# Padding the sample's narrow matmuls and transposes to the full 128 x 128 array in a two-layer attention encoder

## The chip, the core and the metric

One core of one Trainium2 chip runs the whole program in one launch. The metric is device time in microseconds (us). The kernel before takes 1110.06 us, the median of 3 runs (1109.81 to 1110.37).

## What is computed

320 tokens of width 2048 go through two layers: 256 tokens of a prompt and 64 tokens of a sample, whose 128 earlier tokens lie in caches. Cut to what matters:

```python
# layer 0, 16 heads: latent attention, block-causal mask
s = (q . k) * 192**-0.5                  # 128 plain + 64 rotary dimensions
o = softmax(mask(s)) @ v
# layer 1, 16 heads: stick-breaking attention, strictly causal
z = (q . k) * 128**-0.5
log_fail = where(causal, log_sigmoid(-z), 0)
later = cumsum_from_the_right(log_fail) - log_fail
a = where(causal, exp(log_sigmoid(z) + later), 0)
o = a @ v
# both layers
x = x + (o * silu(gate)) @ w_o
```

A sample token attends to 128 past keys and to the 64 own keys of the sample. Those 64 rows and columns are what the change is about. The outputs are the normalised tokens and the new cache entries of both layers.

## The kernel before, in words

Activations are kept transposed, features on the 128 partitions and the 320 tokens along the free axis. Every weight tile is loaded by DMA, split by ScalarE (the high half, L72) and VectorE (the low half, L73), and used in three products in the type float32r: high x high, high x low, low x high (L84, L85, L87; L124 to L126 and L456 to L462 in layer 0). A matmul in plain float32 (own sample keys, own sample values, the last rows of the prompt) is issued as two instructions; the trace therefore counts 32 where there are 16 heads. A transpose is one instruction on TensorE with an identity matrix.

The work of a head is cut into steps in a queue (`steps`); `tick()` takes up one step after each piece of a product, so that the softmax of one head goes on while TensorE works on the products of another. A scheduler in the framework sets the final order of each engine's instructions, close to the order of the program.

Layer 0, `mla_head` (L330), per head:
- `scores` (L335): the scores of the prompt into a PSUM tile `sc`, those of the sample (64 rows, L341) into a part of the PSUM tile `o`; then the softmax. The sample's probabilities lie in `pq`, 64 partitions x 192 keys.
- `transposes` (L371): three full transposes of `p` (L375), then two of `pq`: L376 has 64 rows and 128 columns, L377 64 rows and 64 columns. ScalarE copies the results into `pt` (L382, and L383 for the 64 x 64 corner).
- `values` (L386): three float32r products, then plain float32: L391 (prompt), L392 (sample x past) and L393 (sample x own, contraction over 64 rows).

The own values of the sample lie in `vv[0:TS, 2]`, filled by L468 for each pair of heads.

Layer 1, `sb_head` (L522), per head:
- `scores` (L526): three float32r products (L529), then plain float32: L530 (past keys), L531 (own keys, 64 columns of the array), L532. VectorE clears the 64 rows of the PSUM tile that L531 leaves out (L533); then the softplus chain of ScalarE and VectorE (L535 to L542).
- `sums` (L545): L548 and L551, then two full transposes of `vT` (L560) and one of its last 64 columns (L561); ScalarE copies the results into `vt` (L565, L566).
- `values` (L569): L573 in float32r, then plain float32 L574, L575 (past values) and L576 (own values). `vt` holds zeros in the 64 rows without a key, so L576 has 128 rows already.

```python
pe.transpose(tr[:, 384:448], pq[:, TS:192], ident_t[0:TS, 0:TS])
pe.matmul(o[:, TP:T], vv[0:TS, 2, vs], pt[0:TS, 192:256], start=False, stop=True)
pe.matmul(sc[0:TS, 448:512], kT[:, TP:T], q[:, TP:T], start=False, stop=False)
pe.transpose(tr[0:TS, 256:384], vT[:, TP:T], ident_t)
```

Of the kernel before, what the change touches and what calls it, by code (L numbers as in the profile page):

```python
# [10 lines left out]
F32 = mybir.dt.float32  # L11
F32R = mybir.dt.float32r
AF = mybir.ActivationFunctionType
ALU = mybir.AluOpType
# [3 lines left out]
P = 128  # L18
TP, TS, PAST = 256, 64, 128
T = TP + TS  # L20
# [15 lines left out]
def stream_encoder(  # L36
# [21 lines left out]
    # Work that waits for other engines is cut into steps; one is taken up after each piece of a product.  # L58
# [45 lines left out]
    def gemms(srcs, xh, xl):  # L104
        """The products of a list of tiles, in order; the first three begin together with their first halves,
        so that the last columns of the input may come later."""
        outs = [bank() for _ in srcs[:3]]
        raws = [load(w) for w in srcs[:3]]
        for out, raw in zip(outs, raws):
            half(out, raw, 0, xh, xl)  # L110
        while steps:
            tick()
        for out, raw in zip(outs, raws):
            half(out, raw, 1, xh, xl)
            yield out
        for w in srcs[3:]:
            yield gemm(w, xh, xl)
# [34 lines left out]
    def sum_squares(pool, src, i, acc, name):  # L152
        """acc += src^2"""
        if i == 0:
            s.activation(acc, src, AF.Square)
            return
        sq = pool.tile([P, T], F32, name=name, bufs=2)
        s.activation(sq, src, AF.Square)
        v.tensor_tensor(out=acc, in0=acc, in1=sq, op=ALU.add)

    def inv_rms(pool, ps, n, name, keep=const):
        """1 / sqrt(ps / n + EPS) by the tables and one Newton step."""
        ms = pool.tile([P, T], F32, name="ms")
        r = keep.tile([P, T], F32, name=name)
        t = pool.tile([P, T], F32, name="mt")
        s.activation(t, ps, AF.Ln, bias=eps, scale=1.0 / n)
        s.activation(r, t, AF.Exp, scale=-0.5)
        v.tensor_scalar(ms, ps, 1.0 / n, EPS, op0=ALU.mult, op1=ALU.add)
        v.tensor_tensor(out=t, in0=r, in1=r, op=ALU.mult)
        v.scalar_tensor_tensor(out=t, in0=t, scalar=-0.5, in1=ms, op0=ALU.mult, op1=ALU.mult)  # L170
        v.scalar_tensor_tensor(out=r, in0=t, scalar=1.5, in1=r, op0=ALU.add, op1=ALU.mult)
        return r
# [22 lines left out]
    # ================= layer 0: latent attention =================  # L195
    xh = apool.tile([P, KT, T], F32R, name="ah")
    xl = apool.tile([P, KT, T], F32R, name="al")
    with ExitStack() as stack:
        mp = stack.enter_context(tc.tile_pool(name="mla", bufs=1, reuse_waits="tile"))
        with tc.tile_pool(name="mla_a", bufs=1, reuse_waits="tile") as pa:  # L200
            # The first three tiles go through the inner dimension in step with the arrival of x.
# [60 lines left out]
            # rotary keys: KA = [high; high], KB = [low; chunk mask], against QA = [high; low], QB = [high; chunk]  # L262
# [17 lines left out]
            # rotary key: 64 columns, so that [high | low] of a tile of weights fills the array  # L280
# [43 lines left out]
        # the sample's own latents as [high | low], whose products lie in the two halves of the rows  # L324
# [4 lines left out]

        def mla_head(h, qn, qh, ql, QA, QB, kn, kh, kl, vh, vl, vv, c0):  # L330
            """One head in three steps: scores and softmax, transposes, values."""
# [3 lines left out]
            def scores():  # L335
                sc = pss.tile([P, 512], F32, name="sc")
                o = pso.tile([P, 512], F32, name="o")
                for out, q0, q1, k0, k1 in (
                    (sc[:, 0:128], 0, P, 0, P),
                    (sc[:, 128:384], P, TP, 0, TP),  # L340
                    (o[0:TS, T:512], TP, T, TP, KV),  # L341
                ):
                    q, k = slice(q0, q1), slice(k0, k1)
                    if q0 == 0:
                        pe.matmul(out, qn[:, q], kn, start=True, stop=False)
                    else:
                        q_ = slice(q0 - P, q1 - P)
                        pe.matmul(out, qh[:, q_], kh[:, k], start=True, stop=False)
                        pe.matmul(out, qh[:, q_], kl[:, k], start=False, stop=False)
                        pe.matmul(out, ql[:, q_], kh[:, k], start=False, stop=False)  # L350
                    pe.matmul(out, QA[:, q], KA[:, k], start=False, stop=False)
                    pe.matmul(out, QB[R, q], KB[R, k], start=False, stop=True)
                nm = pb.tile([P, 4], F32, name="nm", bufs=2)
                sm = pb.tile([P, 4], F32, name="sm", bufs=2)
                p = pb.tile([P, 384], F32, name="p", bufs=2)
                pq = pb.tile([TS, 192], F32, name="pq", bufs=2)
                parts = (
                    (p[:, 0:128], sc[:, 0:128], P, 0),
                    (p[:, 128:384], sc[:, 128:384], P, 1),
                    (pq, o[0:TS, T:512], TS, 2),  # L360
                )
                for dst, src, n, i in parts:
                    v.tensor_reduce(out=nm[:n, i : i + 1], in_=src, axis=AX.X, op=ALU.max, negate=True)
                    s.activation(dst, src, AF.Exp, bias=nm[:n, i : i + 1], accum_out=sm[:n, i : i + 1])
                v.reciprocal(sm[:, 0:2], sm[:, 0:2])
                v.reciprocal(sm[:TS, 2:3], sm[:TS, 2:3])
                for dst, src, n, i in parts:
                    v.tensor_scalar(dst, dst, sm[:n, i : i + 1], None, op0=ALU.mult)
                at.update(o=o, p=p, pq=pq)

            def transposes():  # L371
                p, pq = at["p"], at["pq"]
                tr = pst.tile([P, 512], F32, name="tr")
                for j in range(3):
                    pe.transpose(tr[:, j * P : (j + 1) * P], p[:, j * P : (j + 1) * P], ident_t)  # L375
                pe.transpose(tr[:, 384:448], pq[:, TS:192], ident_t[0:TS, 0:TS])  # L376
                pe.transpose(tr[0:TS, 448:512], pq[:, 0:TS], ident_t[0:TS, 0:TS])  # L377
# [4 lines left out]
                s.copy(pt[:, 0:192], tr[:, 256:448])  # L382
                s.copy(pt[0:TS, 192:256], tr[0:TS, 448:512])  # L383
                at.update(ph=ph, pl=pl, pt=pt)

            def values():  # L386
# [4 lines left out]
                pe.matmul(o[:, P:TP], vv[:, 0, vs], pt[:, 0:128], start=False, stop=True)  # L391
                pe.matmul(o[:, TP:T], vv[:, 1, vs], pt[:, 128:192], start=True, stop=False)  # L392
                pe.matmul(o[:, TP:T], vv[0:TS, 2, vs], pt[0:TS, 192:256], start=False, stop=True)  # L393
# [6 lines left out]
        for pair in range(H // 2):  # L400
# [48 lines left out]
            vv = pb.tile([P, 3, 256], F32, name="vv", bufs=2)  # L449
# [32 lines left out]
    # ================= output projection, residual, input of layer 1 =================  # L482
# [15 lines left out]
    # ================= layer 1: stick-breaking attention =================  # L498
    # columns of a score tile: keys 0..127 x queries 0..255 | past x sample | keys 128..255 x queries 128..255 |
    # own x sample (in the first 64 rows; the others hold zeros, which are masked)  # L500
# [10 lines left out]
    kTs, vts = [], []  # L511
    for i in range(2):
        kT = sb.tile([P, T], F32, name=f"kT{i}")
        kTs.append(kT)
        vt = sb.tile([P, 2, P], F32, name=f"vt{i}")
        v.memset(vt[TS:P, 1, :], 0.0)
        vts.append(vt)
# [4 lines left out]
    def sb_head(h, q, qh, ql, kT, kh, kl, vT, g, vt, kp, vp):  # L522
        """One head in three steps: scores and their softplus, sums over later keys, values."""
        at = {}

        def scores():  # L526
# [4 lines left out]
            pe.matmul(sc[0:TS, 448:512], kT[:, TP:T], q[:, TP:T], start=False, stop=False)  # L531
            pe.matmul(sc[:, 320:448], kT[:, P:TP], q[:, P:TP], start=False, stop=True)  # L532
            v.memset(sc[TS:P, 448:512], 0.0)  # L533
# [11 lines left out]
        def sums():  # L545
# [13 lines left out]
            for j in range(2):  # L559
                pe.transpose(tr[:, j * P : (j + 1) * P], vT[:, j * P : (j + 1) * P], ident_t)  # L560
            pe.transpose(tr[0:TS, 256:384], vT[:, TP:T], ident_t)  # L561
# [3 lines left out]
            s.copy(vt[:, 0, :], tr[:, 128:256])  # L565
            s.copy(vt[0:TS, 1, :], tr[0:TS, 256:384])  # L566
            at.update(a=a, pairs=((vh, ah), (vh, al), (vl, ah)))

        def values():  # L569
            a = at["a"]  # L570
# [13 lines left out]
    for h in range(H):  # L584
# [15 lines left out]
        kT, vt = kTs[h % 2], vts[h % 2]  # L600
# [6 lines left out]
        vT = sb.tile([P, T], F32, name="vT", bufs=2)  # L607
        g = sb.tile([P, T], F32, name="g", bufs=2)
        f0, f1, f2 = sb_head(h, q, qh, ql, kT, kh, kl, vT, g, vt, kp[:, h % 4, :], vp[:, h % 4, :])
        steps.extend(([f0], [], [], [f1], [], [f2]))  # L610
        psv = gemm(wsb[4 * h + 2], xh, xl)
        v.tensor_tensor(out=vT, in0=psv, in1=r1, op=ALU.mult)
        nc.gpsimd.dma_start(ov[h], vT)
# [5 lines left out]
    # ================= output projection, residual, final norm =================  # L619
# [54 lines left out]
def _tiles(w):  # L674
    """[K, M] -> [M / 128, partition, K / 128 * 128]: a tile's weights in one run a partition."""
# [69 lines left out]
```

## Time and profile before

| what | value |
|---|---|
| median of 3 runs | 1110.06 us |
| span of the profiled execution, first to last instruction (its own time; no other is given for it) | 1108.3 us |
| TensorE matmul busy (PE) | 1087.4 us, 98% of the span |
| TensorE weight load busy (PEld) | 1072.9 us, 97% |
| VectorE busy (DVE) | 669.1 us, 60% |
| ScalarE busy (ACT) | 582.8 us, 53% |
| DMA queues, largest share of 16 engines | 39.5% |

Busy time of PE is a union of modelled durations: each matmul is shown for some 0.2 to 0.5 us, while the next one starts earlier. So a busy PE can still lose time, and what one matmul costs is read from the distance between the starts of two.

### The profile page before, as it was taken

What the parts mean: (1) busy time and instruction counts of PE and PEld (TensorE: products, weight loads), DVE (VectorE), ACT (ScalarE), POOL (GpSimd) and SP (SyncE); (2) the same over time, 40 slices, a digit from 0 to 9 for tenths busy, and PEclk for the clock granted to TensorE, in tenths of its full rate; (3) what the DMA queues carried; (4) which work ended last, traced back from release to release, by engine and by line L of the source; (5) the groups of instructions that cost most, each with busy time, mean ns of one, the idle gap of its engine ahead of it and who ended that gap; (6) DMA issues with size and microseconds to landing.
All of it is one profiled execution on the core that took longest, in us unless ns stands there. A gap on an engine that the chain in (4) does not pass through costs nothing.

```text
span 1108.3 us, 18683 instructions
## 1 busy us (share of the span) xinstructions
PE 1087.4 (98%) x7484; PEld 1072.9 (97%) x7484; DVE 669.1 (60%) x1355; ACT 582.8 (53%) x1260; POOL 18.8 (2%) x38
## 2 busy tenths in 40 slices
PE   7999999999999999999999999999999999999994
PEld 7999999999999999999999999999999999999994
DVE  7776556786877655555555555555555555555444
ACT  7755555665656544444555545545554545555441
POOL 0000000000000000000000000000000000000000
PEclk9999999999999999999999999999999999999997
DMA  8545443321312554444344443444343434434422
GB/s 304 169 161 185 153 152 100 111 96 58 115 58 77 197 198 169 169 149 156 125 159 151 159 152 138 162 142 154 131 164 127 164 131 160 134 145 153 152 77 95
DMA packets 30552, 159.41 MB, mean 144 GB/s; under 512 B 4264, under 2 KB 8304, under 8 KB 13952
## 3 DMA queue, kind: packets, MB, share of 16 engines
q1 hardware_dynamic: 26912, 151.01, 39.5%
q0 software_dynamic: 1712, 5.98, 1.5%
q10 hardware_dynamic: 1840, 1.22, 0.4%
q8 instruction: 58, 0.95, 0.3%
q14 instruction: 30, 0.25, 0.1%
HBM read 149.59 MB, written 8.60 MB: 143 GB/s over the span
## 4 chain that ended last, share of the span: by engine, by line
PE 97%; DMA 1%; DVE 1%; ACT 0%; issue 0%; DVEq 0%; SPq 0%; ACTq 0%
PE g L84 25%; PE g L87 25%; PE g L85 25%; PE g L124 3%; PE g L126 2%; PE g L125 2%; PE g L460 1%; PE g L461 1%; PE g L462 1%; PE sc L548 1%; PE sc L532 1%; DMA xt<-xT 1%; DVE x L640 1%; PE o L393 1%; PE o L573 1%; PE sc L529 1%
## 5 line engine op out<-in xcount | busy, mean ns | idle before, releaser
L72 ACT CAST whi<-raw 128x512 fp32r<-128x512 f32 (+1 forms) x539 | 309.4, 616 | 319.8 <-PE g L85 243.1
L73 DVE TENSOR_TENSOR wlo<-raw,whi 128x512 fp32r<-128x512 f32 (+1 forms) x539 | 353.3, 682 | 130.0 <-ACT whi L72 118.3
L84 PE MATMUL g<-x2h,whi 128*128 128x320 f32 x1024 | 305.9, 313 | 0.0
L85 PE MATMUL g<-x2l,whi 128*128 128x320 f32 x1024 | 302.1, 309 | 0.0
L84 PE MATMUL g<-ah,whi 128*128 128x320 f32 x848 | 250.9, 310 | 0.0
L85 PE MATMUL g<-al,whi 128*128 128x320 f32 x848 | 250.6, 309 | 0.0
L85 PEld LDWEIGHTS g<-x2l,whi 128*128 128x128 f32 x1024 | 192.4, 188 | 0.0
L84 PEld LDWEIGHTS g<-x2h,whi 128*128 128x128 f32 x1024 | 192.4, 188 | 0.0
L87 PE MATMUL g<-x2h,wlo 128*128 128x320 f32 x1024 | 171.0, 309 | 0.0
L85 PEld LDWEIGHTS g<-al,whi 128*128 128x128 f32 x848 | 159.2, 188 | 0.1
L84 PEld LDWEIGHTS g<-ah,whi 128*128 128x128 f32 x848 | 159.1, 188 | 0.2
L87 PEld LDWEIGHTS g<-x2h,wlo 128*128 128x128 f32 x1024 | 155.5, 188 | 0.0
L87 PE MATMUL g<-ah,wlo 128*128 128x320 f32 x848 | 141.6, 309 | 0.0
L87 PEld LDWEIGHTS g<-ah,wlo 128*128 128x128 f32 x848 | 128.7, 188 | 0.0
L627 DVE TENSOR_TENSOR x<-g,x 128x320 f32<-128x320 f32 x16 | 7.9, 492 | 37.5 <-PE g L87 37.5
L538 DVE SCALAR_TENSOR_TENSOR sp<-sc,sp 128x512 f32<-128x512 f32 x16 | 11.1, 691 | 31.9 <-ACT sp L537 31.9
L124 PE MATMUL g<-cq_h,whi 128*128 128x320 f32 x96 | 30.1, 314 | 0.0
L125 PE MATMUL g<-cq_l,whi 128*128 128x320 f32 x96 | 29.7, 309 | 0.0
L126 PE MATMUL g<-cq_h,wlo 128*128 128x320 f32 x96 | 29.7, 309 | 0.0
L149 ACT CAST ah<-og 128x320 fp32r<-128x320 f32 x32 | 14.7, 460 | 28.4 <-DVE og L395 17.6
L615 DVE TENSOR_TENSOR g<-g,r 128x320 f32<-128x320 f32 x16 | 7.9, 492 | 34.5 <-PE g L87 34.5
L460 PE MATMUL g<-whi,ckv_h 128*128 128x256 f32 x96 | 28.5, 297 | 0.0
(271 smaller groups left out, 1379.2 us busy)
## 6 DMA issues: line engine op xcount, KB each, us to landing
raw<-wsb SPq DMA_DIRECT2D x64, 1024.0 KB, 4.9
raw<-wo SPq DMA_DIRECT2D x32, 1024.0 KB, 4.9
raw<-win SPq DMA_DIRECT2D x21, 1024.0 KB, 5.0
raw<-wmla SPq DMA_DIRECT2D x12, 1024.0 KB, 4.9
xt<-xT SPq DMA_DIRECT2D x16, 160.0 KB, 2.7
ok<-kT POOLq DMA_DIRECT2D x16, 160.0 KB, 2.5
ov<-vT POOLq DMA_DIRECT2D x16, 160.0 KB, 2.1
raw<-win SPq DMA_DIRECT2D x3, 768.0 KB, 8.1
```

The costliest lines, as they stand in the source:

```text
L72: s.copy(hi[:, c], raw[:, c])
L73: v.tensor_tensor(out=lo[:, c], in0=raw[:, c], in1=f32(hi[:, c]), op=ALU.subtract)
L84: pe.matmul(out, hi[:, w], xh[:, k, :], start=k == 0, stop=False)
L85: pe.matmul(out, hi[:, w], xl[:, k, :], start=False, stop=False)
L87: pe.matmul(out, lo[:, i * P : (i + 1) * P], xh[:, k, :], start=False, stop=k == KT - 1)
L124: pe.matmul(out, hi[:, w], xh[:, k, :n], start=k == 0, stop=False)
L125: pe.matmul(out, hi[:, w], xl[:, k, :n], start=False, stop=False)
L126: pe.matmul(out, lo[:, w], xh[:, k, :n], start=False, stop=k == LT - 1)
L149: s.copy(hi, src)
L393: pe.matmul(o[:, TP:T], vv[0:TS, 2, vs], pt[0:TS, 192:256], start=False, stop=True)
L460: pe.matmul(out, ckv_h[:, k, ts], whi[:, w], start=k == 0, stop=False)
L538: v.scalar_tensor_tensor(out=sp, in0=sc, scalar=0.0, in1=sp, op0=ALU.max, op1=ALU.add)
```

## The change

- Layer 0: `pq` becomes two fixed tiles of 128 partitions whose lower 64 rows are set to zero once; the five transposes of a head all take 128 rows and 128 columns, in another order of columns, and overlap in the PSUM tile; one copy of 256 columns replaces the copies L382 and L383. `vv` becomes two fixed tiles whose lower 64 rows of the own values are set to zero once; L393 takes 128 rows.
- Layer 1: `kT` and `vT` become two fixed tiles each of 384 columns, the last 64 of them zero. L531 takes 128 columns of the array, L561 too. The clearing L533 goes. One copy of 256 columns replaces L565 and L566; `vt` becomes an ordinary tile with one buffer.
- The scores of the sample in layer 0 (L341, 64 columns of the array) and the products with 68 rows (L352) stay as they are.

```diff
+        pqs, vvs = [], []
+        for i in range(2):
+            pq = pb.tile([P, 192], F32, name=f"pq{i}")
+            v.memset(pq[TS:P, :], 0.0)
+            pqs.append(pq)
+            vv = pb.tile([P, 3, 256], F32, name=f"vv{i}")
+            v.memset(vv[TS:P, 2, :], 0.0)
+            vvs.append(vv)
...
-                for j in range(3):
-                    pe.transpose(tr[:, j * P : (j + 1) * P], p[:, j * P : (j + 1) * P], ident_t)
-                pe.transpose(tr[:, 384:448], pq[:, TS:192], ident_t[0:TS, 0:TS])
-                pe.transpose(tr[0:TS, 448:512], pq[:, 0:TS], ident_t[0:TS, 0:TS])
+                for c, src in ((0, p[:, 0:P]), (P, p[:, P:TP]), (TP, pq[:, 0:P]), (T, pq[:, TS:192]), (384, p[:, TP:384])):
+                    pe.transpose(tr[:, c : c + P], src, ident_t)
...
-                s.copy(pt[:, 0:192], tr[:, 256:448])
-                s.copy(pt[0:TS, 192:256], tr[0:TS, 448:512])
+                s.copy(pt, tr[:, 256:512])
...
-                pe.matmul(o[:, TP:T], vv[0:TS, 2, vs], pt[0:TS, 192:256], start=False, stop=True)
+                pe.matmul(o[:, TP:T], vv[:, 2, vs], pt[:, 0:64], start=False, stop=True)
...
-        kT = sb.tile([P, T], F32, name=f"kT{i}")
+        kT = sb.tile([P, 3 * P], F32, name=f"kT{i}")
+        v.memset(kT[:, T:], 0.0)
...
-            pe.matmul(sc[0:TS, 448:512], kT[:, TP:T], q[:, TP:T], start=False, stop=False)
+            pe.matmul(sc[:, 448:512], kT[:, TP:], q[:, TP:T], start=False, stop=False)
...
-            v.memset(sc[TS:P, 448:512], 0.0)
...
-            for j in range(2):
+            for j in range(3):
                 pe.transpose(tr[:, j * P : (j + 1) * P], vT[:, j * P : (j + 1) * P], ident_t)
-            pe.transpose(tr[0:TS, 256:384], vT[:, TP:T], ident_t)
...
-            s.copy(vt[:, 0, :], tr[:, 128:256])
-            s.copy(vt[0:TS, 1, :], tr[0:TS, 256:384])
+            vt = sb.tile([P, 2, P], F32, name="vt")
+            s.copy(vt.rearrange("p a c -> p (a c)"), tr[:, 128:384])
```

## Rows read from the trace of the kernel before

**Rows 1.** The page: span, TensorE, chain that ended last; then TensorE's longest wait.
```profile
span 1108.3 us, 18683 instructions
...
PE 1087.4 (98%) x7484; PEld 1072.9 (97%) x7484; DVE 669.1 (60%) x1355; ACT 582.8 (53%) x1260; POOL 18.8 (2%) x38
...
PE 97%; DMA 1%; DVE 1%; ACT 0%; issue 0%; DVEq 0%; SPq 0%; ACTq 0%
...
PE o L84 <- ACT whi L72: 6.1, 2, 5.8
```
**Rows 2.** Timeline of PE, layer 1 values of head 0 (start us, us, instruction).
```profile
515.19 0.39 PE L574 MATMUL o<-a,vt 128*128 128x128 f32 x2
...
515.58 0.39 PE L576 MATMUL o<-a,vt 128*128 128x64 f32 x2
...
516.01 0.30 PE L85 MATMUL g<-x2l,whi 128*128 128x320 f32 x1
```
**Rows 3.** Timeline of PE, layer 1 scores of head 0; then L531's durations, min/median/max.
```profile
495.39 0.33 PE L530 MATMUL sc<-q,kp 128*128 128x64 f32 x2
495.66 0.33 PE L531 MATMUL sc<-q,kT 128*64 128x64 f32 x2
495.91 0.49 PE L532 MATMUL sc<-q,kT 128*128 128x128 f32 x2
...
496.39 0.31 PE L85 MATMUL g<-x2l,whi 128*128 128x320 f32 x1
...
L531 PE MATMUL sc<-q,kT x32: 222/246/270, 495.7 to 966.5; 128*64 128x64 f32 x32
```
**Rows 4.** Timeline of PE, layer 0: last transpose and values of head 15.
```profile
374.12 0.22 PE L377 MATMUL tr<-ident_t,pq 64*64 64x64 f32 x1
...
376.48 0.38 PE L391 MATMUL o<-pt,vv 128*128 128x128 f32 x2
...
376.96 0.43 PE L393 MATMUL o<-pt,vv 64*128 64x64 f32 x2
...
377.57 0.31 PE L85 MATMUL g<-al,whi 128*128 128x320 f32 x1
```
**Rows 5.** Timeline of PE, layer 0 transposes of head 0.
```profile
210.09 0.49 PE L375 MATMUL tr<-ident_t,p 128*128 128x128 f32 x3
210.51 0.27 PE L376 MATMUL tr<-ident_t,pq 64*128 64x64 f32 x1
...
211.07 0.36 PE L125 MATMUL g<-ckv_l,whi 128*128 128x448 f32 x1
211.27 0.36 PE L126 MATMUL g<-ckv_h,wlo 128*128 128x448 f32 x1
```
**Rows 6.** Timeline of PE, layer 1 transposes of head 0.
```profile
507.46 0.38 PE L560 MATMUL tr<-ident_t,vT 128*128 128x128 f32 x2
507.68 0.27 PE L561 MATMUL tr<-ident_t,vT 128*64 128x128 f32 x1
...
507.94 0.30 PE L85 MATMUL g<-x2l,whi 128*128 128x320 f32 x1
```
**Rows 7.** Timeline of ACT and then of PE: layer 0 copies, layer 1 sums.
```profile
376.00 0.31 ACT L382 COPY pt<-tr 128x192 f32<-128x192 f32 x1
376.21 0.20 ACT L383 COPY pt<-tr 64x64 f32<-64x64 f32 x1
...
506.80 0.39 PE L548 MATMUL sc<-sph,triR 128*128 128x512 f32 x1
```
**Rows 8.** Timeline of DVE, layer 1 softplus of head 0.
```profile
496.61 0.11 DVE L533 MEMSET sc<- 64x64 f32 x1
...
501.05 0.68 DVE L150 TENSOR_TENSOR spl<-sp,sph 128x512 fp32r<-128x512 f32 x1
```
**Rows 9.** Timeline of PEld, weight loads of L531 and of L576, head 0.
```profile
495.65 0.19 PEld L531 LDWEIGHTS sc<-q,kT 128*64 128x64 f32 x2
...
515.52 0.30 PEld L576 LDWEIGHTS o<-a,vt 128*128 128x128 f32 x2
```

More of the change, by code (lines that the diff above doesn't have):

```diff
@@ L355, in scores @@
                 p = pb.tile([P, 384], F32, name="p", bufs=2)
-                pq = pb.tile([TS, 192], F32, name="pq", bufs=2)
+                pq = pqs[h % 2]
                 parts = (
@@ L359, in scores @@
                     (p[:, 128:384], sc[:, 128:384], P, 1),
-                    (pq, o[0:TS, T:512], TS, 2),
+                    (pq[0:TS, :], o[0:TS, T:512], TS, 2),
                 )
@@ L390, in values @@
                 pe.matmul(o[:, 0:TP], vl[:, vs], ph, start=False, stop=False)
-                pe.matmul(o[:, P:TP], vv[:, 0, vs], pt[:, 0:128], start=False, stop=True)
-                pe.matmul(o[:, TP:T], vv[:, 1, vs], pt[:, 128:192], start=True, stop=False)
-                pe.matmul(o[:, TP:T], vv[0:TS, 2, vs], pt[0:TS, 192:256], start=False, stop=True)
+                pe.matmul(o[:, P:TP], vv[:, 0, vs], pt[:, 128:256], start=False, stop=True)
+                pe.matmul(o[:, TP:T], vv[:, 1, vs], pt[:, 64:128], start=True, stop=False)
+                pe.matmul(o[:, TP:T], vv[:, 2, vs], pt[:, 0:64], start=False, stop=True)
                 og = pb.tile([P, T], F32, name="og")
@@ L448, in stream_encoder @@
             vl = pb.tile([P, 256], F32R, name="vl", bufs=2)
-            vv = pb.tile([P, 3, 256], F32, name="vv", bufs=2)
+            vv = vvs[pair % 2]
             for i, t0 in ((0, P), (None, 0), (2, None), (1, T)):
@@ L510, in stream_encoder, with sb_head @@
     s.activation(minusR, ones, AF.Copy, scale=-1.0)
-    kTs, vts = [], []
+    kTs, vTs = [], []
     for i in range(2):
-        kT = sb.tile([P, T], F32, name=f"kT{i}")
+        kT = sb.tile([P, 3 * P], F32, name=f"kT{i}")
+        v.memset(kT[:, T:], 0.0)
         kTs.append(kT)
-        vt = sb.tile([P, 2, P], F32, name=f"vt{i}")
-        v.memset(vt[TS:P, 1, :], 0.0)
-        vts.append(vt)
+        vT = sb.tile([P, 3 * P], F32, name=f"vT{i}")
+        v.memset(vT[:, T:], 0.0)
+        vTs.append(vT)
     oh = apool.tile([P, KT, T], F32R, name="ah")
     ol = apool.tile([P, KT, T], F32R, name="al")
-    def sb_head(h, q, qh, ql, kT, kh, kl, vT, g, vt, kp, vp):
+    def sb_head(h, q, qh, ql, kT, kh, kl, vT, g, kp, vp):
         at = {}
@@ L564, in sums @@
             plain_split(vh, vl, tr[:, 0:128])
-            s.copy(vt[:, 0, :], tr[:, 128:256])
-            s.copy(vt[0:TS, 1, :], tr[0:TS, 256:384])
-            at.update(a=a, pairs=((vh, ah), (vh, al), (vl, ah)))
+            vt = sb.tile([P, 2, P], F32, name="vt")
+            s.copy(vt.rearrange("p a c -> p (a c)"), tr[:, 128:384])
+            at.update(a=a, vt=vt, pairs=((vh, ah), (vh, al), (vl, ah)))
         def values():
-            a = at["a"]
+            a, vt = at["a"], at["vt"]
             o = pso.tile([P, 512], F32, name="o")
@@ L599, in stream_encoder @@
         plain_split(qh, ql, q[:, 0:TP])
-        kT, vt = kTs[h % 2], vts[h % 2]
+        kT, vT = kTs[h % 2], vTs[h % 2]
         psk = gemm(wsb[4 * h + 1], xh, xl)
@@ L606, in stream_encoder @@
         plain_split(kh, kl, kT[:, 0:P])
-        vT = sb.tile([P, T], F32, name="vT", bufs=2)
         g = sb.tile([P, T], F32, name="g", bufs=2)
-        f0, f1, f2 = sb_head(h, q, qh, ql, kT, kh, kl, vT, g, vt, kp[:, h % 4, :], vp[:, h % 4, :])
+        f0, f1, f2 = sb_head(h, q, qh, ql, kT, kh, kl, vT, g, kp[:, h % 4, :], vp[:, h % 4, :])
         steps.extend(([f0], [], [], [f1], [], [f2]))
         psv = gemm(wsb[4 * h + 2], xh, xl)
-        v.tensor_tensor(out=vT, in0=psv, in1=r1, op=ALU.mult)
-        nc.gpsimd.dma_start(ov[h], vT)
+        v.tensor_tensor(out=vT[:, 0:T], in0=psv, in1=r1, op=ALU.mult)
+        nc.gpsimd.dma_start(ov[h], vT[:, 0:T])
         psg = gemm(wsb[4 * h + 3], xh, xl)
```

## The prediction, written before the changed kernel was run

> **What bounds the kernel now.** I read the page first: the span is 1108.3 us, PE is busy for 98% of it, and the chain of work that ended last is PE for 97% [rows 1]. Then the waits of PE: the longest, 6.1 us, belongs to the first products (a weight half that is late at the start), and the heads have none [rows 1]. So TensorE sets the time, and a microsecond taken out of its stream of instructions comes off the end, as long as nobody makes it wait. Busy time can't show where that stream is thin, because the drawn matmuls overlap. So I read the timeline of PE around the instructions that the diff touches, and compare distances between starts.
>
> The measure is a block of the kernel before in which every matmul takes the whole array: the layer 1 values. From the first L574 to L85, the second matmul of the following product, it takes 516.01 - 515.19 = 0.82 us for six plain float32 instructions (two with 128 moving columns, four with 64) and one product matmul of 320 columns [rows 2].
>
> The layer 1 scores hold the same six shapes in another order, four with 64 moving columns and two with 128, and the same product behind, except that L531 loads only 64 columns of the array. From L530 to the second product matmul they take 496.39 - 495.39 = 1.00 us [rows 3]. The visible gap lies before L531 (0.27 us for two L530) and behind it. The 32 instructions of L531 have the same few durations from first to last [rows 3], so I take head 0 for all 16.
>
> The layer 0 values are again the same six shapes, but L393 takes 64 rows. From L391 to the second product matmul: 377.57 - 376.48 = 1.09 us [rows 4], which I take for all 16 heads too.
>
> The layer 0 transposes: from the first L375 to L125, the second matmul behind, 211.07 - 210.09 = 0.98 us; three transposes take 0.42 up to the start of L376, where the change of shape falls [rows 5].
>
> **The change part by part.**
>
> *Layer 1 scores.* After the change this is six full instructions and the product: 0.82 us by [rows 2] against 1.00, so 0.18 us a head, 16 x 0.18 = 2.9 us. L531's wider weights are inside the 0.82, since L576 loads 128 columns there.
>
> *Layer 0 values.* 1.09 - 0.82 = 0.27 us a head, 16 x 0.27 = 4.3 us. Most heads are followed by a product of 256 columns instead of 320, which shifts both sides alike.
>
> *Layer 0 transposes.* Full transposes come every 0.11 us: two L560 take 507.68 - 507.46 = 0.22 [rows 6]. Five take 0.55; the first product matmul behind them takes 0.20, as 211.27 - 211.07 shows for that shape [rows 5]. That is 0.75 against 0.98: 0.23 us a head, 3.7 us in all.
>
> *Layer 1 transposes.* L561 takes 64 columns before and 128 after. It follows L560 without a gap, and L85 comes 507.94 - 507.68 = 0.26 us later, one transpose of 0.11 and one product matmul of about 0.15 [rows 6]. Nothing is lost there now, so nothing is won: 0. The bound on the other side is a weight load twice as wide, 0.055 us by the difference in [rows 9], 0.9 us in all; the 0.11 us of the transpose in front of it covers that.
>
> At this place a rule can be weighed against a row. L561 shows no gap although its tile differs from its neighbours' [rows 6], while L376, L393 and L531 do. The Trainium skill, TensorEngine Tiling (Array Packing), Key Properties, says that changing the tiling mode drains the engine, and lists 128 x 64 as a mode of its own. By that, L561 would lose what the others lose, and padding it would win some 0.23 us a head more. The row says it does not; the sum goes by the row.
>
> *The sample's scores in layer 0* keep their 64 columns, so they neither cost nor win anything.
>
> *ScalarE.* L382 and L383 take 0.31 + 0.20 us [rows 7]; one copy of 256 columns lies between 0.31 and 0.51, and by columns near 0.37. L565 and L566 merge likewise. ScalarE is 53% busy and gets less to do: 0 for the path, apart from the last pair below. The single buffer of `vt` makes the copy of one head wait for L576 of the head before, which has run a whole head earlier: 0.
>
> *VectorE.* The 16 clearings L533 go, 0.11 us each [rows 8]. They stand ahead of the softplus chain, whose last result ends at 501.05 + 0.68 = 501.73 while L548, which reads it, starts at 506.80 [rows 7, 8]: over 5 us of cover, so their going gives 0. New are eight clearings at the start of the two layers, in place of two. At 0.11 to 0.3 us each (scaled from L533 by columns) they cost some 1.5 us of an engine that is idle 40% of the time: 0, at most that 1.5 if the low half of a weight queued behind them came late.
>
> *What is late next.* In the last pair of layer 0 the copies into `pt` end at 376.21 + 0.20 = 376.41 and L391 starts at 376.48 [rows 4, 7]: 0.07 us of margin. Between that head's transposes and its values lie the values of head 14, whose 0.27 us go. TensorE then comes too early and waits, in both heads of the pair. I put 0.2 us a head, 0.4 in all; the bounds are 0 (the merged copy is shorter) and 1.0. In the other pairs more products lie between the two steps.
>
> **Sum:** 2.9 + 4.3 + 3.7 - 0.4 = 10.5 us. The span goes from 1108.3 to 1097.8. The median of the runs is 1.8 us above the span, which I leave as it is: 1110.06 - 10.5 = **1099.6 us**, a gain of 0.9%.
>
> **The rivals.**
> 1. *Part of the gaps stays or comes back as waits.* Were the order of the last pair to shift so that PE waits out the whole chain from the last transpose, which starts at 374.12 [rows 4], to the end of the copies into `pt` at 376.41, 2.3 us, in both heads, 4.6 us would be lost instead of 0.4: 1103.8. For it: the margin of 0.07 us. Against: products stood between the steps before, and can again. 5%.
> 2. *More comes back.* If L561's narrow tile costs too and the 0.26 us hide it, 16 x 0.23 = 3.7 us more go: 1095.9. This is what the drain rule named above would give. Against: L561 starts 0.11 us after the transpose before it [rows 6]. 3%.
> 3. *The gaps do not hang on the shape.* They would then come from the change of type from float32r to float32 or from short matmuls, which stay, and the change does not do what it says: about 1110. Against: L574 to L576 have the same types and lengths, and no gap [rows 2]. 4%.
> 4. *Slower.* The gaps stay as in rival 3, and the wider weights show. Two loads of L531 take 0.19 us, two of 128 columns 0.30 [rows 9], so 0.11 more a head there, 0.055 for L377 and 0.055 for L561: 0.22 us a head, 3.5 us, 1113.6. It decides as soon as less than 0.22 us of gap goes per pair of heads (one of each layer), where the forecast has 0.68. The Trainium skill, TensorE: Matmul & The Clock Gate, LDWEIGHTS (loading the stationary operand), says that a load goes by its columns and not by its rows; the rows agree for columns. Against: in [rows 2] loads of 128 columns are in the 0.82 us already. 3%.
>
> **How the numbers follow.** The forecast has 85%, the rivals 15%. Starts are read to 0.01 us; over three blocks and 16 heads that is about half a microsecond. With the last pair's 0 to 1.0 us and 0.3 us between runs, the forecast's own range is 1098.4 to 1100.8. In the scores the two long instructions come last instead of first, which can hide one more load of 0.06 us a head, 1 us: down to 1097.4. Half of rival 1 takes the top to 1101.6. A measurement of this kernel tells 0.2%, 2.2 us, from no change. Forecast and rivals 1 and 2 are faster by more: 0.93. Rival 3 is the same: 0.04. Rival 4 is slower: 0.03.
>
> **What would show it.** Right: in the timeline of PE the layer 0 and layer 1 blocks each take 0.82 us up to the second product matmul, the five transposes start 0.11 us apart, the layer 1 transposes look as before, and PE waits only in the last pair of layer 0, for `pt` or `pl`. Wrong: L531 or L393 still start about 0.2 us after their neighbours; PE gets waits inside the heads; or the gaps are gone and the span has not shortened, which would mean that something beside TensorE paces the products.

## The result and the profile after

The changed kernel takes 1099.74 us (median; 1099.41 to 1099.97) where the kernel before takes 1110.21 (1109.81 to 1110.61) beside it: a ratio of 0.9905, 95% interval 0.9891 to 0.9919, so 10.5 us less. The forecast was 1099.6 us.

The page of the changed kernel, span and TensorE, then the chain that ended last, then TensorE's waits:

```profile
span 1097.6 us, 18604 instructions
...
PE 1076.9 (98%) x7484; PEld 1070.5 (98%) x7484; DVE 667.8 (61%) x1345; ACT 578.5 (53%) x1228; POOL 18.7 (2%) x38
...
PE 97%; DMA 1%; DVE 1%; ACT 0%; issue 0%; DVEq 0%; SPq 0%
...
PE o L84 <- ACT whi L72: 5.7, 1, 5.7
PE sc L630 <- ACT sq L640: 1.1, 1, 1.1
```

These answer to [rows 1]. TensorE executes as many matmuls as before, 7484, is as busy in share, and still bounds the kernel; its busy time went down by 10.5 us, as much as the runs did. Its count did not change, so the time came out of the distances between matmuls. Three starts split the span: the first product of layer 0's heads (L124), the first product of layer 1 (L84), and the sum of squares behind both layers (L624, in the changed kernel L630). Timeline of PE, before and then after:

```profile
183.93 0.31 PE L124 MATMUL g<-cq_h,whi 128*128 128x320 f32 x1
477.15 0.31 PE L84 MATMUL g<-x2h,whi 128*128 128x320 f32 x1
1093.94 0.81 PE L624 MATMUL sc<-sq,ones 128*128 128x320 f32 x2 [1.08 <-ACT sq L634]
```

```profile
183.44 0.31 PE L124 MATMUL g<-cq_h,whi 128*128 128x320 f32 x1
468.86 0.31 PE L84 MATMUL g<-x2h,whi 128*128 128x320 f32 x1
1082.94 0.81 PE L630 MATMUL sc<-sq,ones 128*128 128x320 f32 x2 [1.08 <-ACT sq L640]
```

Layer 0, from L124 to L84, went from 293.22 to 285.42 us, 7.8 less; layer 1, from L84 on, from 616.79 to 614.08, 2.7 less. Together that is the 10.5 us. The span fell by 10.8 us before rounding: another 0.5 us lie before L124, where the change touches nothing and where the profiles of this document differ by up to a microsecond (L124 starts between 183.28 and 184.25 us), and behind the last product it took some 0.2 us longer.

The blocks of the prediction, in the timeline of PE (start us, us, instruction). First the layer 1 scores, where L540 is the padded product of the own keys:

```profile
487.11 0.33 PE L539 MATMUL sc<-q,kp 128*128 128x64 f32 x2
487.28 0.39 PE L540 MATMUL sc<-q,kT 128*128 128x64 f32 x2
...
487.93 0.31 PE L85 MATMUL g<-x2l,whi 128*128 128x320 f32 x1
```

From L539 to the second product matmul it is 487.93 - 487.11 = 0.82 us, where [rows 3] have 1.00. L540 starts 0.17 us after L539, where L531 came 0.27 after L530.

The layer 0 values of head 15, to be read beside [rows 4]:

```profile
368.03 0.38 PE L399 MATMUL o<-pt,vv 128*128 128x128 f32 x2
368.25 0.33 PE L400 MATMUL o<-pt,vv 128*128 128x64 f32 x2
368.42 0.39 PE L401 MATMUL o<-pt,vv 128*128 128x64 f32 x2
...
368.84 0.45 PE L84 MATMUL g<-ah,whi 128*128 128x320 f32 x2
```

Here it is 368.84 - 368.03 = 0.81 us instead of 1.09, within 0.01 us of the block of full matmuls [rows 2].

The layer 0 transposes of head 0, beside [rows 5]:

```profile
209.59 0.38 PE L386 MATMUL tr<-ident_t,p 128*128 128x128 f32 x2
209.81 0.38 PE L386 MATMUL tr<-ident_t,pq 128*128 128x128 f32 x2
210.03 0.27 PE L386 MATMUL tr<-ident_t,p 128*128 128x128 f32 x1
...
210.35 0.37 PE L125 MATMUL g<-ckv_l,whi 128*128 128x448 f32 x1
```

Five transposes 0.11 us apart, and 210.35 - 209.59 = 0.76 us to the second product matmul instead of 0.98.

The layer 1 transposes, beside [rows 6]; the third of them is the widened one:

```profile
499.01 0.49 PE L568 MATMUL tr<-ident_t,vT 128*128 128x128 f32 x3
...
499.48 0.30 PE L85 MATMUL g<-x2l,whi 128*128 128x320 f32 x1
```

499.48 - 499.01 = 0.47 us; before it was 507.94 - 507.46 = 0.48. Nothing was there to win.

### The profile page after: what moved, and what is told of

Read it like the earlier page. It is cut to its first block, busy times and chain, and to the rows that moved or that the text cites. A ratio compares the mean times of both kernels' runs of the same rounds, so it can differ in the third digit from the quotient of the medians.

```text
span 1097.6 us, 18604 instructions
## 1 busy us (share of the span) xinstructions
PE 1076.9 (98%) x7484; PEld 1070.5 (98%) x7484; DVE 667.8 (61%) x1345; ACT 578.5 (53%) x1228; POOL 18.7 (2%) x38
## 4 chain that ended last, share of the span: by engine, by line
PE 97%; DMA 1%; DVE 1%; ACT 0%; issue 0%; DVEq 0%; SPq 0%
PE g L84 25%; PE g L87 25%; PE g L85 25%; PE g L124 2%; PE g L126 2%; PE g L125 2%; PE g L468 1%; PE g L469 1%; PE g L470 1%; PE tr L386 1%; PE sc L556 1%; DVE x L646 1%; DMA xt<-xT 1%; PE o L580 1%; PE sc L538 1%; PE tr L568 0%
## 5 line engine op out<-in xcount | busy, mean ns | idle before, releaser
L84 PE MATMUL g<-x2h,whi 128*128 128x320 f32 x1024 | 306.1, 313 | 0.0
L85 PE MATMUL g<-x2l,whi 128*128 128x320 f32 x1024 | 302.2, 309 | 0.0
L84 PE MATMUL g<-ah,whi 128*128 128x320 f32 x848 | 250.8, 310 | 0.0
L85 PE MATMUL g<-al,whi 128*128 128x320 f32 x848 | 250.4, 309 | 0.0
L85 PEld LDWEIGHTS g<-x2l,whi 128*128 128x128 f32 x1024 | 192.5, 188 | 0.0
L84 PEld LDWEIGHTS g<-x2h,whi 128*128 128x128 f32 x1024 | 192.5, 188 | 0.0
L85 PEld LDWEIGHTS g<-al,whi 128*128 128x128 f32 x848 | 159.2, 188 | 0.1
L84 PEld LDWEIGHTS g<-ah,whi 128*128 128x128 f32 x848 | 159.1, 188 | 0.1
L124 PE MATMUL g<-cq_h,whi 128*128 128x320 f32 x96 | 30.1, 314 | 0.0
L125 PE MATMUL g<-cq_l,whi 128*128 128x320 f32 x96 | 29.7, 309 | 0.0
L609 DVE TENSOR_TENSOR kT<-g,r 128x320 f32<-128x320 f32 x16 | 7.9, 491 | 34.0 <-PE g L87 34.0
L603 DVE TENSOR_TENSOR q<-g,r1s 128x320 f32<-128x320 f32 x16 | 7.9, 491 | 32.4 <-PE g L87 32.3
```

The lines of the kernel that those rows point to most:

```text
L84: pe.matmul(out, hi[:, w], xh[:, k, :], start=k == 0, stop=False)
L85: pe.matmul(out, hi[:, w], xl[:, k, :], start=False, stop=False)
L124: pe.matmul(out, hi[:, w], xh[:, k, :n], start=k == 0, stop=False)
L125: pe.matmul(out, hi[:, w], xl[:, k, :n], start=False, stop=False)
```

## The experiments

The theory: TensorE loses some 0.2 to 0.3 us whenever it goes into a narrower shape of the array and back out (a visit), and the narrower shapes here are operands of 64 rows, or 64 columns in plain float32. The rivals: one part of the change carries the gain; the gap belongs to the narrow instructions themselves, or to the change of type; the lighter ScalarE and VectorE have a share in it. The kernels below were timed in five rounds against the kernel before.

### The parts, each alone on the kernel before

`k_scores`:

```diff
-        kT = sb.tile([P, T], F32, name=f"kT{i}")
+        kT = sb.tile([P, 3 * P], F32, name=f"kT{i}")
+        v.memset(kT[:, T:], 0.0)
...
-            pe.matmul(sc[0:TS, 448:512], kT[:, TP:T], q[:, TP:T], start=False, stop=False)
+            pe.matmul(sc[:, 448:512], kT[:, TP:], q[:, TP:T], start=False, stop=False)
...
-            v.memset(sc[TS:P, 448:512], 0.0)
```

> The kernel before with only the layer 1 own keys padded: L531 takes 128 columns and L533 goes. Theory (a plain float32 matmul narrower than the array costs TensorE a gap on the way in and out): the scores block shrinks from 1.00 to 0.82 us a head, 16 x 0.18 = 2.8 us less, about 1107.4 where the kernel before takes 1110.2. Rival (the gap belongs to the change of type or to short matmuls): no gain, or up to 1.8 us more for the wider weight loads.

Measured: 1107.44 us against 1110.17, ratio 0.9977 (0.9968 to 0.9986): 2.7 us less.

`k_values` (with `vv` and `pt` as two fixed tiles each, whose added rows are zeroed once):

```diff
-                pe.matmul(o[:, TP:T], vv[0:TS, 2, vs], pt[0:TS, 192:256], start=False, stop=True)
+                pe.matmul(o[:, TP:T], vv[0:128, 2, vs], pt[0:128, 192:256], start=False, stop=True)
```

> The kernel before with only the layer 0 own values padded: L393 takes 128 rows (the rows added to pt and vv are zero). Theory: 1.09 to 0.82 us a head, 4.3 us less, about 1105.9 where the kernel before takes 1110.2. Rival (gap not from the shape): 1110.2.

Measured: 1106.09 against 1110.17, ratio 0.9964 (0.9952 to 0.9977): 4.1 us less.

`k_transposes` (with `pq` as two fixed tiles of 128 partitions, and `pt` read in the new order of columns; L393 keeps its 64 rows):

```diff
-                for j in range(3):
-                    pe.transpose(tr[:, j * P : (j + 1) * P], p[:, j * P : (j + 1) * P], ident_t)
-                pe.transpose(tr[:, 384:448], pq[:, TS:192], ident_t[0:TS, 0:TS])
-                pe.transpose(tr[0:TS, 448:512], pq[:, 0:TS], ident_t[0:TS, 0:TS])
+                for c, src in ((0, p[:, 0:P]), (P, p[:, P:TP]), (TP, pq[:, 0:P]), (T, pq[:, TS:192]), (384, p[:, TP:384])):
+                    pe.transpose(tr[:, c : c + P], src, ident_t)
...
-                s.copy(pt[:, 0:192], tr[:, 256:448])
-                s.copy(pt[0:TS, 192:256], tr[0:TS, 448:512])
+                s.copy(pt, tr[:, 256:512])
```

> The kernel before with only the layer 0 transposes full: five of 128 x 128, one copy into pt. Theory: 0.98 to 0.75 us a head, 3.7 us less, about 1106.5 where the kernel before takes 1110.2; with k_scores and k_values the three parts add up to the whole change. Rival (one part carries it all, or the parts overlap): the three gains do not add up to the 10.5 us of the whole.

Measured: 1106.90 against 1110.17, ratio 0.9970 (0.9959 to 0.9981): 3.3 us less.

The three together: 2.7 + 4.1 + 3.3 = 10.1 us, and the whole change 10.5. The parts add up within the intervals, and no single one carries the gain.

`k_vt` (with `vT` as two fixed tiles of 384 columns, the last 64 set to zero once):

```diff
-            pe.transpose(tr[0:TS, 256:384], vT[:, TP:T], ident_t)
+            pe.transpose(tr[:, 256:384], vT[:, TP:], ident_t)
```

> The kernel before with only the layer 1 transpose of the own values widened from 64 to 128 columns (L561). Theory by the row: no gap there, 0 +- 0.5 us, about 1110.2. Rival (64 columns are a tiling mode of their own in a transpose as well, as the drain rule has it): 3.7 us less, 1106.5. Other rival (the wider load shows): 0.9 us more, 1111.1.

Measured: 1110.16 against 1110.17, ratio 1.0 (0.9992 to 1.0009). The timeline of PE of this kernel:

```profile
507.09 0.38 PE L563 MATMUL tr<-ident_t,vT 128*128 128x128 f32 x2
507.31 0.27 PE L564 MATMUL tr<-ident_t,vT 128*128 128x128 f32 x1
...
507.57 0.30 PE L85 MATMUL g<-x2l,whi 128*128 128x320 f32 x1
```

0.48 us from L563 to L85, as in [rows 6]. Layer 1 in this profile, from its first L84 (476.78 us) to L627 (1093.57), takes the same 616.79 us as in the kernel before. So a transpose with 64 columns and 128 rows is not a narrow shape for the engine, and the wider load does not show. Both rivals of this part fall: the 3.7 us lie outside the interval, and the 0.9 us, at its edge, are ruled out by the timeline.

### Two visits in place of one

`k_alternate` executes the same five transposes as the kernel before, in another order:

```diff
+                pe.transpose(tr[:, 0:P], p[:, 0:P], ident_t)
                 pe.transpose(tr[:, 384:448], pq[:, TS:192], ident_t[0:TS, 0:TS])
+                pe.transpose(tr[:, P : 2 * P], p[:, P : 2 * P], ident_t)
                 pe.transpose(tr[0:TS, 448:512], pq[:, 0:TS], ident_t[0:TS, 0:TS])
+                pe.transpose(tr[:, 2 * P : 3 * P], p[:, 2 * P : 3 * P], ident_t)
```

(the loop over three full ones goes).

> The kernel before with its five layer 0 transposes in another order: full, 64 rows (L376), full, 64 rows (L377), full. Same instructions, two visits to the narrow shape where there was one. Theory (each visit costs, whatever its length): 16 x 0.23 = 3.7 us more, about 1113.9 where the kernel before takes 1110.2. Rival (the narrow instructions themselves are slow): no change, 1110.2.

Measured: 1114.00 against 1110.26, ratio 1.0035 (1.0022 to 1.0047): 3.7 us more. Its timeline of PE for head 0:

```profile
210.40 0.27 PE L374 MATMUL tr<-ident_t,p 128*128 128x128 f32 x1
210.60 0.27 PE L375 MATMUL tr<-ident_t,pq 64*128 64x64 f32 x1
210.81 0.33 PE L376 MATMUL tr<-ident_t,p 128*128 128x128 f32 x1
211.06 0.24 PE L377 MATMUL tr<-ident_t,pq 64*64 64x64 f32 x1
211.24 0.33 PE L378 MATMUL tr<-ident_t,p 128*128 128x128 f32 x1
...
211.61 0.36 PE L125 MATMUL g<-ckv_l,whi 128*128 128x448 f32 x1
```

From the first transpose to L125: 211.61 - 210.40 = 1.21 us with two visits, 0.98 with one [rows 5], 0.76 with none. Each visit costs 0.22 to 0.23 us. Full and narrow transposes alike start 0.18 to 0.25 us after the one before them here, where full ones follow each other after 0.11, and where in the kernel before the second narrow one (L377) starts 0.11 us after the first (210.62 and 210.51). With the same instructions in both kernels, the narrow ones are not slow in themselves: the price is on the change of shape.

### How many rows count as narrow

`k_rows96` is `k_values` with

```diff
-                pe.matmul(o[:, TP:T], vv[0:128, 2, vs], pt[0:128, 192:256], start=False, stop=True)
+                pe.matmul(o[:, TP:T], vv[0:96, 2, vs], pt[0:96, 192:256], start=False, stop=True)
```

> As k_values, but L393 takes 96 rows in place of 128. Theory (only up to 64 rows are another shape, since L352 with 68 rows shows no gap): the same as k_values, 4.3 us less than the kernel before, about 1105.9. Rival (anything short of 128 rows costs): 1110.2.

Measured: 1105.85 against 1110.26, ratio 0.9960 (0.9947 to 0.9974): 4.4 us less, as with 128 rows. Its timeline of PE:

```profile
217.09 0.39 PE L399 MATMUL o<-pt,vv 128*128 128x128 f32 x2
217.31 0.33 PE L400 MATMUL o<-pt,vv 128*128 128x64 f32 x2
217.48 0.39 PE L401 MATMUL o<-pt,vv 96*128 96x64 f32 x2
217.68 0.36 PE L464 MATMUL g<-whi,own 128*128 128x256 f32 x1
217.88 0.28 PE L465 MATMUL g<-wlo,own 128*128 128x256 f32 x1
```

0.79 us, with no gap before or behind 96 rows, where the kernel before takes 1.07 for this head (L391 at 217.30, the second product matmul at 218.37; the product behind has 256 columns here). So it is not being short of 128 that costs; 64 rows cost, 96 do not. Types and lengths in this block are those of the kernel before, so the gap is not one of type or of length. The 68 rows of L352, in float32r, cost nothing either: in the kernel before the last of them starts 0.09 us behind its neighbour, and the next matmul 0.09 behind it (202.43, 202.52, 202.61).

### The work beside TensorE put back

`k_offpath`, on the changed kernel:

```diff
+            v.memset(sc[TS:P, 448:512], 0.0)
             sp = sb.tile([P, 512], F32, name="sp")
...
-                s.copy(pt, tr[:, 256:512])
+                s.copy(pt[:, 64:256], tr[:, 320:512])
+                s.copy(pt[:, 0:64], tr[:, 256:320])
...
-            s.copy(vt.rearrange("p a c -> p (a c)"), tr[:, 128:384])
+            s.copy(vt[:, 0, :], tr[:, 128:256])
+            s.copy(vt[:, 1, :], tr[:, 256:384])
```

> The changed kernel with the work beside TensorE put back: the clearing of 64 rows of the score tile in layer 1, and two copies in place of one in both layers. Theory (all of it is covered): the time of the changed kernel, 1099.7, within 0.5 us. Rival (part of the gain is the lighter ScalarE and VectorE): 1100.5 to 1102.

Measured: 1100.19 against 1110.26, ratio 0.9909 (0.9895 to 0.9922), beside 0.9905 for the changed kernel. That is the upper edge of what the theory allowed. The 0.45 us between the two medians are inside the intervals, which would hide more than a microsecond. The profiles tell more; their spans are 0.9 us apart, and 0.7 of it lie before the first head (L124 starts at 184.14 us instead of 183.44). Timelines of PE and ACT:

```profile
366.48 0.49 PE L400 MATMUL o<-pt,vv 128*128 128x128 f32 x2
366.80 0.38 PE L386 MATMUL tr<-ident_t,p 128*128 128x128 f32 x2
...
469.96 0.31 PE L84 MATMUL g<-x2h,whi 128*128 128x320 f32 x1
...
1084.03 0.81 PE L633 MATMUL sc<-sq,ones 128*128 128x320 f32 x2 [1.08 <-ACT sq L643]
...
366.10 0.32 ACT L391 COPY pt<-tr 128x192 f32<-128x192 f32 x1 [0.82 <-DVE pl L150]
```

Layer 1 takes 1084.03 - 469.96 = 614.07 us, as in the changed kernel (614.08): the clearing and the second copy cost nothing there. Layer 0 takes 469.96 - 184.14 = 285.82 us, 0.4 more than the 285.42 of the changed kernel (285.43 in a second profile of it, `k_after_again`). Nearly all of it lies in the last pair of heads: up to that pair's first transposes it is 0.04 us (364.17 - 184.14 against 363.43 - 183.44). There L400 starts 0.06 us behind the end of the first copy into `pt` (366.10 + 0.32 = 366.42), and its two instructions take 0.32 us up to the next matmul instead of 0.22; in the other head of the pair the starts are the same distance apart (copy at 368.83, L400 at 369.20, the next at 369.52). These two delays make 0.2 us. So some 0.4 us of the gain hang on the single copy or on the order that the scheduler chose with it, which this run does not tell apart. The other 10 us need nothing from ScalarE and VectorE.

### 64 columns in another type

`k_own_r`, on the changed kernel, takes the own keys' scores as three products of halves in float32r, with 64 columns of the array:

```diff
-            pe.matmul(sc[:, 448:512], kT[:, TP:], q[:, TP:T], start=False, stop=False)
+            for k_, q_ in ((khs, qhs), (khs, qls), (kls, qhs)):
+                pe.matmul(sc[0:TS, 448:512], k_, q_, start=False, stop=False)
...
+            v.memset(sc[TS:P, 448:512], 0.0)
...
+        plain_split(qhs, qls, q[:, TP:T])
...
+        plain_split(khs, kls, kT[:, TP:T])
```

> The changed kernel, but the layer 1 scores of the own keys as three products in float32r of high and low halves, with 64 columns of the array, in place of the padded float32 matmul; the halves are made by ScalarE and VectorE, and the 64 rows left out are cleared again. Theory (64 columns are a shape of their own only in plain float32, since the float32r scores of layer 0 with 64 columns show no gap): no gap, three loads of 0.055 us in place of two of 0.11, 0 to 0.8 us less than the changed kernel, 1098.9 to 1099.7. Rival (64 columns cost in any type but a transpose): the gap comes back, about 2.9 us more than the changed kernel, 1102.6.

Measured: 1099.05 against 1110.26, ratio 0.9899 (0.9885 to 0.9912). It was run again beside the changed kernel on one chip:

> The changed kernel again, beside the next one on the same chip: about 1099.7.

> The kernel of k_own_r again, beside the changed kernel. Its scores block took 0.768 us a head in the first run and that of the changed kernel 0.820. If that carries through to the end: 16 x 0.052 = 0.8 us less than the changed kernel, about 1098.9. If the extra splits on ScalarE and VectorE take it back: no difference.

Measured: the changed kernel 1099.75 (1099.53 to 1100.13), ratio 0.9905 (0.9888 to 0.9921); `k_own_r` 1098.68 (1098.34 to 1098.99), ratio 0.9895 (0.9880 to 0.9910). The ranges of the two lie apart, by 1.1 us between medians. The timeline of PE of `k_own_r` in the second run, then of its weight loads:

```profile
487.47 0.33 PE L539 MATMUL sc<-q,kp 128*128 128x64 f32 x2
487.62 0.22 PE L541 MATMUL sc<-qhs,khs 128*64 128x64 f32 x1
487.67 0.22 PE L541 MATMUL sc<-qls,khs 128*64 128x64 f32 x1
487.73 0.22 PE L541 MATMUL sc<-qhs,kls 128*64 128x64 f32 x1
487.79 0.47 PE L542 MATMUL sc<-q,kT 128*128 128x128 f32 x2
...
488.24 0.31 PE L85 MATMUL g<-x2l,whi 128*128 128x320 f32 x1
```

```profile
487.59 0.14 PEld L541 LDWEIGHTS sc<-qhs,khs 128*64 128x64 f32 x1
487.64 0.14 PEld L541 LDWEIGHTS sc<-qls,khs 128*64 128x64 f32 x1
487.70 0.14 PEld L541 LDWEIGHTS sc<-qhs,kls 128*64 128x64 f32 x1
```

The shape is that of L531 before, 128*64, in the same place, and the gap is not there: the block takes 488.24 - 487.47 = 0.77 us. So 64 columns are a narrow shape in plain float32 and not in float32r. The three loads start 0.05 to 0.06 us apart, half of the 0.11 us of full ones, and their matmuls follow at that pace; that is where the block gets under the 0.82 us of the padded one: 16 x 0.05 = 0.8 us. Layer 1 confirms it: 613.22 us from the first L84 (469.23) to L638 (1082.45), where `k_after_again` beside it takes 614.08 (469.32 to 1083.40). What is left of the 1.1 us, 0.2, lies outside the blocks and is not explained. This version beats the changed kernel by little, 0.1%.

## Why the prediction was right, point by point

- *TensorE paces the kernel; what is lost between its matmuls comes off the end.* Right. The two layers got shorter by 10.5 us in the timeline, the runs by 10.5. One reading was off without harm: the 6.1 us in [rows 1] are two waits together, the longest 5.8, and a wait of 1.1 us at L624, behind both layers, is as long after the change.
- *Layer 1 scores, 0.18 us a head, 2.9 us.* Right: the block takes 0.82 us, layer 1 got 2.7 us shorter, and the part alone gave 2.7.
- *Layer 0 values, 0.27 us a head, 4.3 us.* Right: 0.81 us instead of 1.09, the part alone 4.1, with 96 rows 4.4.
- *Layer 0 transposes, 0.23 us a head, 3.7 us.* Right in the trace (0.76 us). Alone the part gave 3.3, with 3.7 inside its interval (2.1 to 4.6 us).
- *Layer 1 transposes, 0.* Right, and shown by `k_vt`. The Trainium skill, TensorEngine Tiling (Array Packing), Key Properties, has every change of tiling mode drain the engine. The runs show a loss at the change of shape for 64 rows and for 64 columns in plain float32, and none for 64 columns in a transpose or in float32r. Whether the loss is such a drain, and which mode an instruction was put in, the profiles do not show.
- *Copies, clearings and buffers beside TensorE, 0 apart from the last pair.* Right in layer 1, to 0.01 us in `k_offpath`; in layer 0 the copies, or the order that came with them, are worth some 0.4 us, nearly all in the last pair, where the prediction had its doubt. One reading was off in its favour: the last result of the softplus chain, `spl`, is read by the L548 at 507.03 us, not by the one at 506.80, which reads `sph`.
- *0.4 us given back in the last pair of layer 0.* Right in kind, half in size: layer 0 got 7.8 us shorter, where 4.3 + 3.7 = 8.0 less 0.4 make 7.6. Only the first head of the pair shows a loss, and not where the sum put it. The scheduler ordered that stretch anew, and L396 and L397 follow hard on the halves `ph` and `pl` (the latter named among the signs), not L399 on `pt`. Timelines of PE, ACT and DVE of the changed kernel:

```profile
364.60 0.39 PE L396 MATMUL o<-ph,vh 128*128 128x256 f32 x1
364.82 0.31 PE L84 MATMUL g<-ah,whi 128*128 128x320 f32 x1
...
365.40 0.36 PE L397 MATMUL o<-pl,vh 128*128 128x256 f32 x1
365.60 0.28 PE L398 MATMUL o<-ph,vl 128*128 128x256 f32 x1
365.72 0.31 PE L84 MATMUL g<-ah,whi 128*128 128x320 f32 x1
...
364.17 0.37 ACT L149 CAST ph<-tr 128x256 fp32r<-128x256 f32 x1 [0.52 <-PE tr L386]
...
364.91 0.42 DVE L150 TENSOR_TENSOR pl<-tr,ph 128x256 fp32r<-128x256 f32 x1
```

  `ph` ends at 364.54 and L396 starts at 364.60; `pl` ends at 365.33 and L397 starts at 365.40. Behind each, the next matmul comes after 0.22 and 0.20 us where the same shape elsewhere takes 0.12 (L398). That is 0.18 us for one head, near the 0.2 us a head that was put down; in the second head L396 to L399 come at their usual distances. That these two delays come from the halves is inferred from the times; the list of waits does not show it, since the drawn matmuls overlap.
- *The sum, 10.5 us.* The mechanism was right; the hit to a tenth was luck. Layer 0 gave 0.2 us more than was summed (7.8 for 7.6) and layer 1 0.2 less (2.7 for 2.9), and the two cancel.
- *The rivals.* Waits that eat the gain: the order of the last pair did shift, but no wait of 2.3 us a head came of it. Another 3.7 us at L561 fell with `k_vt`. That the gap comes from type or length fell with `k_rows96`, where both are the same and the gap is gone, and with `k_own_r`, which changes type twice without a gap. That wider loads would make it slower fell with `k_vt` and the 0.82 us of the scores; the loads do cost what was said, 0.055 us for 64 columns more, but in the padded blocks that is paid inside the 0.82.

## What to carry to other kernels

A lone plain float32 matmul or transpose with 64 rows, or a plain float32 matmul with 64 columns, set among full ones, cost here 0.18 to 0.27 us for the visit, as much as its own work or more. (Rows between 64 and 68, fewer than 64, and 64 rows in float32r were not run.) Pad it with zeros that are written once, or at least put the narrow ones next to each other. Where TensorE is 98% busy, compare the starts of neighbouring matmuls: a block elsewhere in the same trace with the same lengths in full shape gives the price of the change before it is made.

## What had not been expected

Of this the prediction has only that L561 shows no gap; the theories of the later runs forecast the rest, the third as 0 to 0.8 us.

- The price is paid per visit and adds up evenly: none, one and two visits took 0.76, 0.98 and 1.21 us for the same five transposes.
- 64 columns behave by type: a gap in plain float32 (L531), none in a transpose (L561) and none in float32r (L541 of `k_own_r`).
- Three float32r matmuls with 64 columns of weights and 64 moving columns take less time than one padded plain float32 matmul (two instructions): the six-matmul block of 0.82 us became 0.77, with three products in place of one. The loads, half as wide and at half the distance, account for it as far as the rows show.
